# Two-block network with sixteen experts: blocks of 64 in the triangular inverses, part of the convolution and of the masks on GpSimd, output weights loaded into the ring's places

## The chip, the cores and the metric

One core of a Trainium2 chip. The time is device microseconds of one execution, from the median of several. A single profiled execution has its own time; the span is from its first to its last instruction.

## The reference

Two blocks on 256 tokens of width 1024, all in float32. The first (Fourier mixing, neighbourhood attention, an MLP) isn't touched. The second is:

```python
h = rms_norm_2(x, norm_mix_g[l])
p = h @ w_in[l]
q, pc, pr = jnp.split(p, [ATT_WIDTH, ATT_WIDTH + 2 * CONV_WIDTH], axis=-1)
o_att = memory_cross_attention(q, mem_n, w_mk[l], w_mv[l])
o_conv = conformer_conv(pc, conv_w[l], ...)        # gate, 31 taps over 384 channels, layer norm, silu
o_rwkv = rwkv7_bidirectional(pr, shift_mu[l], ...)
x = x + jnp.concatenate([o_att, o_conv, o_rwkv], axis=-1) @ w_out[l]
x = x + expert_choice_ffn(rms_norm_2(x, norm_ffn_g[l]), w_router[l], w_e_gate[l], w_e_up[l], w_e_down[l])
```

The recurrence of `rwkv7_bidirectional`, for six heads of 64, once forward and once backward over the 256 tokens, is

```python
sa = jnp.einsum('bhij,bhj->bhi', state, -kk_t)
state = state * w_t[..., None, :] + sa[..., :, None] * (kk_t * a_t)[..., None, :] + v_t[..., :, None] * k_t[..., None, :]
y_t = jnp.einsum('bhij,bhj->bhi', state, r_t)
```

`expert_choice_ffn` gives each of 16 experts its 32 best tokens; an expert's three matrices are 1024x1024 each.

## The kernel before, in words

The second block runs in `branches`. Its stages overlap, and generators that are advanced in turn (`weave`) write the program in that order; a framework then orders the instructions of each engine.

Projections, attention and convolution (to about 569 us). `w_in` comes in pieces as `raw`, is split into two parts (`split`) by ScalarE and VectorE, and TensorE multiplies (`pw`). Meanwhile the decays, the normalised keys `kkn` and the operands `ex`, `aa` of both directions are made (`decays`, `keys`, `start`). The convolution has 3 x 128 channels in rows and the 256 tokens in columns. Of `cacc[:, 2]` ScalarE makes a product for each tap (`cp`) and TensorE adds them up by a product with the identity (`pconv`, generator `cpe`); `cacc[:, 0]` and `cacc[:, 1]` are 31 taps each on VectorE, a `scalar_tensor_tensor` of 128x256 per tap (`conv`, generator `ct`). GpSimd does little.

The recurrence, in two chunks of 128 tokens, two directions d, and three pairs of heads i, so four 128x128 matrices a pair (2 chunks by 2 heads). `scores(d, i, z)`: products of the operands (`psab`) are masked on VectorE to `LM` (z = 0, kept) or to `LK` (z = 1, one buffer `LM1`, read by `values` for `prh` and `py`). `diagonal` takes the 16x16 blocks of the triangular matrix out (`tm`, then a reduction to `N`), and GpSimd adds the identity. `blocks16` inverts these blocks in 15 steps, one product `prep` and two small VectorE operations each, and spreads the result as a block-diagonal `Gm` of 128 columns. `levels` doubles the blocks twice (16 to 32, 32 to 64): `pp` from the transposed inverse `Tm`, a mask by VectorE to `P`, `pg` to the next `Gm`, and `turn`, four transposes for each of three pairs (`pt`), all as full 128x128 products. A third level joins the two 64 blocks with 64x64 products. `finish(d)` solves (`pu`, `pzz`, `prz`, `py`).

The order: scores of direction 0, then `blocks16(0)` with the scores of direction 1 and convolution, `levels(0)` with `blocks16(1)`, and `levels(1)` with `finish(0)`, the later scores of direction 1 and `bonus`. Then the output weights are read (six loads in `rows0`, `rows1`), and the output products run among the steps of `finish(1)`.

The experts' weights come through a ring of places in SBUF. A place is `wide` (4096 columns) or single (2048). `ring_room` opens places in the space of pools that have closed, `ring_load` issues as many loads on SyncE's queue as there are free places, in the fixed order of the pieces, and `ring_free` gives a place back and loads again. The lists RING, RING0 to RING3 say how many places a point opens and of what size: RING (1, 1, 1, 1) behind the projections, RING0 behind the third level, RING1 behind `finish(1)`, RING2 behind `branches`. A load can't start before the last reader of the space is done.

In the profile's names L277 and L274 are ScalarE copies and activations, L283 VectorE operations of two tensors, L286 those on GpSimd, L290 and L292 operations with scalars, L295 `scalar_tensor_tensor`, L298 products, L302 transposes, L335 weight loads and L1916 the ring's loads.

## Time and profile before

| | us |
|---|---|
| median of 3 runs | 1173.91 (1173.83 to 1174.78) |
| the profiled execution | 1177.93 |
| its span | 1176.2 |
| TensorE busy in the span | 1047.3 (89%) |
| VectorE busy | 509.4 (43%) |
| ScalarE busy | 417.7 (36%) |
| GpSimd busy | 45.7 (4%) |

A share of busy time is a mean over stages with different limits, so the stages are read one by one, by windows. Idle time of an engine counts only where the next engine on the chain waits for it. In the rows, `x` and a number is a count; a matmul in float32 shows as two records per product of full width (a transpose as one).

### The profile page before, as it was taken

The page shows a single profiled execution, that of the slowest core. Times are in us where ns is not written, and L with a number is a line of the kernel's source. Part 1 is how long each engine was busy: PE and PEld are TensorE (multiplying, and loading weights), DVE is VectorE, ACT ScalarE, POOL GpSimd, SP SyncE. Part 2 cuts the span into 40 slices and gives each one's busy share as a digit, 9 for nine tenths or more (in the row PEclk, how much of TensorE's full clock was granted, in tenths as well). Part 3 has the DMA queues.
Part 4 walks back from the last instruction along what each step waited for, and adds up shares of the span by engine and source line. Part 5 has one row for each costly group of instructions (what it writes and reads, how often), then busy time and mean ns, then how long its engine had stood idle before and what let it go on. Part 6 is the DMA issues. An engine that isn't in the chain of part 4 may idle for free.

```text
span 1176.2 us, 19111 instructions
## 1 busy us (share of the span) xinstructions
PE 1047.3 (89%) x8188; PEld 754.7 (64%) x8188; DVE 509.4 (43%) x964; ACT 417.7 (36%) x718; POOL 45.7 (4%) x50
## 2 busy tenths in 40 slices
PE   5999999999999999999989998989877877777776
PEld 4886676899999999898679886434322322222223
DVE  3544356586555555669888555212111111111102
ACT  4542368656444444576324533102000000000003
POOL 0000000021000000101310002000000000000000
PEclk9999999999999999999889998999998798788896
DMA  9874446555555553431300269999999999999995
GB/s 361 359 274 167 179 167 211 176 183 182 205 182 182 192 191 115 158 109 36 143 1 2 109 249 373 425 419 395 429 427 426 426 426 427 427 426 427 427 426 236
DMA packets 34964, 313.86 MB, mean 267 GB/s; under 512 B 4800, under 2 KB 5568, under 8 KB 9152
## 3 DMA queue, kind: packets, MB, share of 16 engines
q1 hardware_dynamic: 34880, 312.65, 66.5%
q8 instruction: 64, 1.05, 0.4%
q14 instruction: 20, 0.16, 0.0%
HBM read 311.59 MB, written 1.05 MB: 266 GB/s over the span
## 4 chain that ended last, share of the span: by engine, by line
PE 69%; DMA 19%; DVE 6%; ACT 4%; issue 1%; POOL 1%; SPq 0%; ACTq 0%; POOLq 0%; DVEq 0%
PE pw L298 22%; DMA ew<-in_w_e_up_dram 12%; PE pd L298 10%; PE acc L298 9%; PE pgu L298 6%; DMA ew<-in_w_e_down_dram 5%; PE pv L298 2%; PE pada L298 2%; PE pg L298 1%; PE pp L298 1%; PE py L298 1%; DVE split L283 1%; PE prep L298 1%; ACT split L277 1%; DMA raw<-in_w_branch_gate_dram 1%; PE pt L302 1%
## 5 line engine op out<-in xcount | busy, mean ns | idle before, releaser
L283 DVE TENSOR_TENSOR split<-raw,split 128x1024 fp32r<-128x1024 f32 (+2 forms) x148 | 177.1, 1203 | 116.2 <-ACT split L277 115.7
L277 ACT ACTIVATE split<-raw 128x1024 fp32r<-128x1024 f32 (+2 forms) x148 | 152.1, 1033 | 133.3 <-PE pw L298 74.4
L298 PE MATMUL pgu<-ew,XE 128*32 128x256 f32 x2048 | 146.5, 430 | 57.4 <-DMA ew<-in_w_e_up_dram 56.6
L298 PE MATMUL pd<-ew,hidT 128*32 128x512 f32 (+2 forms) x560 | 151.5, 594 | 11.2 <-DVE hidT L2140 6.2
L298 PEld LDWEIGHTS pgu<-ew,XE 128*32 128x32 f32 x2048 | 67.7, 120 | 127.8 <-DMA ew<-in_w_e_up_dram 69.5
L298 PEld LDWEIGHTS pd<-ew,hidT 128*32 128x32 f32 x560 | 40.9, 117 | 111.1 <-issue 96.6
L298 PE MATMUL acc<-uh,split 128*128 128x256 f32 x512 | 94.7, 283 | 0.0
L298 PE MATMUL pw<-h2h,split 128*128 128x256 f32 x512 | 92.9, 280 | 0.0
L295 DVE SCALAR_TENSOR_TENSOR hid<-pgu,rs,hid 128x256 f32<-128x256 f32 x16 | 7.7, 484 | 191.2 <-ACT hid L274 191.2
L295 DVE SCALAR_TENSOR_TENSOR ye<-pd,ig,ye 128x512 fp32r<-128x512 f32 (+2 forms) x35 | 24.6, 705 | 144.9 <-ACT ye L274 143.4
L274 ACT ACTIVATE hid<-pgu,rs 128x256 f32<-128x256 f32 x16 | 7.6, 473 | 216.5 <-PE pgu L298 216.5
L274 ACT ACTIVATE ye<-pd,ig 128x512 fp32r<-128x512 f32 (+2 forms) x35 | 22.8, 651 | 166.4 <-PE pd L298 166.3
L298 PEld LDWEIGHTS acc<-uh,split 128*128 128x128 f32 x512 | 80.8, 192 | 0.0
L298 PEld LDWEIGHTS pw<-h2h,split 128*128 128x128 f32 x512 | 79.3, 188 | 0.0
L298 PE MATMUL acc<-ul,split 128*128 128x256 f32 x256 | 72.5, 283 | 0.0
L298 PE MATMUL pw<-h2l,split 128*128 128x256 f32 x256 | 71.4, 279 | 0.0
L298 PE MATMUL pw<-hmh,split 128*128 128x256 f32 x320 | 62.4, 292 | 0.0
L298 PE MATMUL pw<-hxh,split 128*128 128x256 f32 x320 | 61.7, 286 | 0.1
L298 PEld LDWEIGHTS pw<-hxh,split 128*128 128x128 f32 x320 | 50.0, 188 | 9.5 <-issue 8.1
L298 PEld LDWEIGHTS pw<-hmh,split 128*128 128x128 f32 x320 | 51.5, 195 | 1.7 <-DVE u L283 0.5
L298 PEld LDWEIGHTS acc<-ul,split 128*128 128x128 f32 x256 | 49.0, 191 | 0.2 <-DVE ul L283 0.2
L298 PEld LDWEIGHTS pw<-h2l,split 128*128 128x128 f32 x256 | 48.0, 187 | 0.0
(441 smaller groups left out, 1731.3 us busy)
## 6 DMA issues: line engine op xcount, KB each, us to landing
ew<-in_w_e_up_dram SPq DMA_DIRECT2D x28, 2048.0 KB, 18.5
ew<-in_w_e_down_dram SPq DMA_DIRECT2D x28, 2048.0 KB, 19.0
ew<-in_w_e_gate_dram SPq DMA_DIRECT2D x27, 2048.0 KB, 22.0
raw<-in_w_mlp_dram SPq DMA_DIRECT2D x32, 1024.0 KB, 4.8
raw<-in_w_ada_dram SPq DMA_DIRECT2D x24, 1024.0 KB, 5.7
raw<-in_w_in_dram SPq DMA_DIRECT2D x18, 1024.0 KB, 4.9
ew<-in_w_e_gate_dram SPq DMA_DIRECT2D x10, 1024.0 KB, 11.9
raw<-in_w_branch_gate_dram SPq DMA_DIRECT2D x8, 1024.0 KB, 4.8
```

Of the source, the lines that this page charges most:

```text
L274: self.nc.scalar.activation(out, in_, func, **kw)
L277: self.nc.scalar.activation(out, in_, AF.Copy)
L283: self.nc.vector.tensor_tensor(out=out, in0=a, in1=b, op=op)
L295: self.nc.vector.scalar_tensor_tensor(out=out, in0=a, scalar=s, in1=b, op0=op0, op1=op1)
L298: self.nc.tensor.matmul(out, lhsT, rhs, start=start, stop=stop, **kw)
L302: self.nc.tensor.transpose(out, in_, self.ident[0:k, 0:k])
```

## The change

1. `conv_pool` (new): of `cacc[:, 1]` 18 of the 31 taps (from TAPS = 13) are made by ScalarE as products `cq` (two buffers) and added up in `chalf` by GpSimd, during the projections. VectorE's taps of that row begin from `chalf` and stop at 13.
2. `scores` with z = 1: ScalarE copies `psab` and GpSimd multiplies by the mask; `LM1` has two buffers.
3. `diagonal`: only the four 32x32 squares on the diagonal are multiplied, one operation of 32 partitions each, and `N` is one addition of two halves.
4. `Gm`, `Tm` and `P` hold only the 64x64 blocks on the diagonal, stacked (64 columns for a matrix instead of 128). A group of four 128x128 products becomes eight 64x64 products in the two diagonal quadrants. The transposed inverse comes from `P` and the inverse directly (`turned`), beside `pg`, and not by a transpose afterwards; the first is still a product with the identity. In the second doubling the result goes into `whole`, whose off-diagonal quadrant the third level fills.
5. The output weights are loaded packed into the two wide places of RING, now (2, 2), where the scores begin; the expert pieces that were loaded there go out after the pools close (RING_ and RING0). The output products' first steps are advanced in the last eight steps of `levels(1)`.

```diff
-RING, RING0, RING1, RING2, RING3 = (1, 1, 1, 1), (2, 2, 2, 2, 1, 1), (1, 1), (2, 2), (1,)
+TAPS = 13
+
+RING, RING_, RING0, RING1, RING2, RING3 = (2, 2), (1, 1), (2, 2, 2, 2, 1, 1), (1, 1), (2, 2), (1,)
...
+        half = rb.tile([128, 256], F32, name="chalf")
+
+        def conv_pool():
+
+            for t in range(TAPS, 31):
+                x, g = u[:, 1, t:t + 256], cw[:, t, 1:2]
+                if t == TAPS:
+                    self.act(half, x, AF.Identity, scale=g, bias=self.v("conv_b_2", 1))
+                else:
+                    p_ = pj.tile([128, 256], F32, name="cq", tag="cq", bufs=2)
+                    self.act(p_, x, AF.Copy, scale=g)
+                    self.tp(half, half, p_, ALU.add)
+                if t % 2:
+                    yield
...
-        for g in (dec, cd, cd, dec, cd, ma, cd, dec, cd, ma, cd, None, prd, dec, prd, ma, prd, dec, prd, ma,
+        for g in (dec, cd, cd, dec, cd, ma, cd, dec, cd, ma, cd, None, prd, dec, cpool, cpool, prd, ma, cpool, cpool,
+                  prd, dec, cpool, cpool, prd, ma, cpool, cpool, cpool,
...
-        self.ring_load()
+        lent = list(self.free)
+        self.free.clear()
+        rows0, rows1 = {}, {}
+        store = [pool.tile([128, 4096], F32, tag=tag, name="raw", bufs=1) for pool, tag in lent]
+        for n in range(4):
+            rows0[256 * n] = self.wload("w_out_2", 0, 640, 256 * n, 256 * n + 256, raw=store[n // 2][:, n % 2 * 1280:])
+        for n in range(2):
+            rows1[512 * n] = self.wload("w_out_2", 640, 1024, 512 * n, 512 * n + 512, raw=store[n][:, 2560:])
...
-            for i in range(2):
-                self.ts(cacc[:, i], u[:, i, 0:256], cw[:, 0, i:i + 1], ALU.mult, self.v("conv_b_2", i), ALU.add)
-                for t in range(1, 31):
+            for i, n in ((0, 31), (1, TAPS)):
...
+                    self.stt(cacc[:, 1], x, g, half, ALU.mult, ALU.add)
+                for t in range(1, n):
...
-                self.tt(lm.rearrange("p y (j e) t -> p e j y t", e=2)[:, e],
-                        ps[e].rearrange("p (j y t) -> p j y t", j=2, y=2),
-                        mst[d][:, None].to_broadcast([128, 2, 2, 128]), ALU.mult)
+                if z:
+                    self.cpa(o, x)
+                    self.tp(o, o, m, ALU.mult)
+                else:
+                    self.tt(o, x, m, ALU.mult)
...
-            tm = wk2.tile([128, 4, 128], F32, tag="tm", name="tm", bufs=1)
-            self.tt(tm, L, bm[:, None, :].to_broadcast([128, 4, 128]), ALU.mult)
-            nc.vector.tensor_reduce(out=N[d][:, 4 * i:4 * i + 4],
-                                    in_=tm.rearrange("p n (b c) -> p n c b", b=8), op=ALU.add, axis=AX)
+            tm = wk2.tile([128, 4, 32], F32, tag="tm", name="tm", bufs=2)
+            for b in range(4):
+                q = slice(32 * b, 32 * b + 32)
+                self.tt(tm[q], L[q, :, q], bm[q, None, q].to_broadcast([32, 4, 32]), ALU.mult)
+            self.tt(N[d][:, 4 * i:4 * i + 4], tm[:, :, 0:16], tm[:, :, 16:32], ALU.add)
...
-                    for z in range(4):
-                        self.mm(ps[:, z], LM[d, i][:, 0, z], T_[d, i][:, z], True, True)
+                    for z in range(4):
+                        for q in hs:
+                            self.mm(ps[q, z], LM[d, i][q, 0, z, q], T_[d, i][q, z], True, True)
...
-                    for z in range(4):
-                        self.mm(ps[:, z], p1[i][:, z], G[d, i][:, z], True, True)
-                    G[d, i] = next(gms)
-                    self.cpa(G[d, i], ps)
+                    for z in range(4):
+                        for q in hs:
+                            self.mm(ps[q, z], p1[i][q, z], G[d, i][q, z], True, True)
+                    turned(d, i, [p1[i][q] for q in hs], [a] if n else hs)
...
-                turn(d)
-                yield
...
-        self.go(lv)
+        prepare(2)
+        for n, _ in enumerate(lv):
+            if n < 8:
+                next(op)
```

Three places in the order of the two programs show how instructions moved. ScalarE during the projections, around the keys (`cq` are the products for GpSimd, `kkn` the keys, `pr` a projection with its shift), before:

```order
L277 ACTIVATE split_5586<-raw_5526 128x1024
L274 ACTIVATE kkn_5052<-pr_4839,vec_73 128x256
L277 ACTIVATE split_5629<-raw_5627 128x1024
L274 ACTIVATE pr_4839<-pad0_4840,mu01_4820 128x256 x2
L277 ACTIVATE om_4790<-pom_5177 128x256
L274 ACTIVATE kkn_5052<-pr_4839,vec_73 128x256 x2
L274 ACTIVATE LM5_5512<-kkn_5052 128x768
L277 ACTIVATE split_5681<-raw_5627 128x1024
```

The same stretch, with the change:

```order
L280 ACTIVATE kkn_5052<-pr_4839,vec_73 128x256
L280 ACTIVATE cq_5480<-u_4835,vec_73 128x256
L280 ACTIVATE cq_5483<-u_4835,vec_73 128x256
L283 ACTIVATE split_5636<-raw_5576 128x1024
L280 ACTIVATE pr_4839<-pad0_4840,mu01_4820 128x256 x2
L283 ACTIVATE om_4790<-pom_5178 128x256
L280 ACTIVATE cq_5541<-u_4835,vec_73 128x256
L280 ACTIVATE cq_5544<-u_4835,vec_73 128x256
L283 ACTIVATE split_5679<-raw_5677 128x1024
L280 ACTIVATE cq_5547<-u_4835,vec_73 128x256
L280 ACTIVATE cq_5550<-u_4835,vec_73 128x256
L280 ACTIVATE kkn_5052<-pr_4839,vec_73 128x256
```

Pairs of products for GpSimd now stand between the splits and ahead of each `kkn`, and each needs a buffer that a GpSimd addition frees. TensorE in `levels(0)`, from the first turn on (`pt`, `pp`, `pg` as above; `prep` belongs to `blocks16(1)`), before:

```order
L302 MATMUL pt1_6115<-cm_75,Gm0_5810 128x128 x4
L302 MATMUL pt1_6122<-cm_75,Gm1_5811 128x128 x4
L302 MATMUL pt1_6129<-cm_75,Gm2_5812 128x128 x4
L298 MATMUL pp1_6142<-Tm_6120,LM0_5804 128x128 x4
L298 MATMUL pp1_6158<-Tm_6127,LM1_5805 128x128 x4
L298 MATMUL pp1_6172<-Tm_6134,LM2_5806 128x128 x4
L298 MATMUL prep_6151<-N_5799,sel_5786 128x192
L298 MATMUL prep_6165<-N_5799,sel_5786 128x192
L298 MATMUL prep_6179<-N_5799,sel_5786 128x192
L298 MATMUL pg1_6186<-Gm0_5810,P1_6147 128x128 x4
L298 MATMUL prep_6192<-N_5799,sel_5786 128x192
L298 MATMUL pg1_6199<-Gm1_5811,P1_6163 128x128 x4
```

The same place, with the change:

```order
L304 MATMUL pp1_6274<-Tm_6222,LM2_5853 64x64 x8
L304 MATMUL pt1_6301<-P1_6245,Gm0_5863 64x64 x8
L304 MATMUL pt1_6329<-P1_6265,Gm1_5864 64x64 x2
L304 MATMUL prep_6249<-N_5846,sel_5833 128x192
L304 MATMUL prep_6267<-N_5846,sel_5833 128x192
L304 MATMUL prep_6285<-N_5846,sel_5833 128x192
L304 MATMUL pg1_6292<-Gm0_5863,P1_6245 64x64 x8
L304 MATMUL prep_6313<-N_5846,sel_5833 128x192
L304 MATMUL pg1_6320<-Gm1_5864,P1_6265 64x64 x8
L304 MATMUL pt1_6329<-P1_6265,Gm1_5864 64x64 x6
L304 MATMUL prep_6341<-N_5846,sel_5833 128x192
L304 MATMUL pg1_6348<-Gm2_5865,P1_6283 64x64 x8
```

The groups are now of 64x64 products, `pt` stands beside `pg`, and full products (`prep`) alternate with small ones. In the second direction the mask of the first later score was VectorE's, before:

```order
L283 TENSOR_TENSOR P1_6448<-pp1_6443,cr_4817 128x512
L283 TENSOR_TENSOR LM1_6462<-psab_6463,cr_4817 128x2x2x128
L283 TENSOR_TENSOR LM1_6462<-psab_6464,cr_4817 128x2x2x128
L283 TENSOR_TENSOR vv_4838<-vv_4838,pm_6473 128x256
L295 SCALAR_TENSOR_TENSOR bn_6521<-kds_5055,vec_73,pr_4839 128x256
```

ScalarE now has the two copies of that mask, with GpSimd's multiply behind each:

```order
L283 ACTIVATE Tm_6615<-pt1_6606 128x256
L283 ACTIVATE LM1_6647<-psab_6648 128x2x2x128
L283 ACTIVATE kkn_5052<-pu_6639 128x3x128
L280 ACT_TABLE_LOAD
L280 ACTIVATE aa0_5045<-cacc_5056 128x768
L283 ACTIVATE LM1_6647<-psab_6649 128x2x2x128
L280 ACTIVATE gate_5051<-gate_5051,vec_73 128x256
L283 ACTIVATE bt1_5847<-pkt_6690 128x256
```

The second copy stands behind a table load and a sigmoid.

## Rows read from the trace of the kernel before

**Rows 1.** Windows: us, busy us of PE, PEld, DVE, ACT, POOL, then PEclk, DMA share, GB/s.

```profile
549.00:569.00 20.00, 17.06 (x88) 13.57 (x87) 19.17 (x29) 9.19 (x23) 9.73 (x5) 0.91 0.33 128
581.00:617.00 36.00, 32.11 (x184) 26.21 (x185) 29.95 (x78) 9.33 (x21) 4.08 (x3) 0.81 0.01 1
637.00:665.00 28.00, 27.97 (x228) 21.86 (x227) 17.41 (x34) 11.76 (x22) 0.00 (x0) 1.00 0.01 1
665.00:707.00 42.00, 41.78 (x373) 36.82 (x372) 22.20 (x36) 19.53 (x35) 0.00 (x0) 1.00 0.63 251
709.00:1160.00 451.00, 357.65 (x2893) 152.31 (x2895) 66.24 (x160) 45.62 (x81) 7.14 (x7) 0.90 1.00 422
```

**Rows 2.** Timeline of SyncE's issues: start us, us, engine, line, operation, tile, count.

```profile
707.76 1.59 SPq L1916 DMA_DIRECT2D ew<-in_w_e_gate_dram  x2
```

**Rows 3.** Timeline of GpSimd; in square brackets idle time before and its releaser.

```profile
550.72 3.68 POOL L286 TENSOR_TENSOR ex<-pr,ex 128x768 f32<-128x768 f32 x2 [76.03 <-DVE stm L290]
...
572.97 1.27 POOL L1558 TENSOR_TENSOR LM<-LM,cm 128x512 f32<-128x512 f32 x1 [6.06 <-DVE tm L283]
...
710.50 0.73 POOL L286 TENSOR_TENSOR km<-sq 128x256 f32<-128x256 f32 x1 [96.36 <-ACT sq L274]
```

**Rows 4.** Timeline of VectorE, same columns.

```profile
546.58 0.69 DVE L283 TENSOR_TENSOR pad<-pw,rs 128x512 f32<-128x512 f32 x1 [1.36 <-PE pw L298]
...
551.48 3.39 DVE L292 TENSOR_SCALAR LM<-aa,vec,oneka 128x256 f32<-128x256 f32 x3
...
561.93 1.05 DVE L292 TENSOR_SCALAR LM<-aa,vec,oneka 128x256 f32<-128x256 f32 x3
```

**Rows 5.** Chain that ended last, 572 to 617 us: start us, us, what.

```profile
576.72 0.94 DVE N L1556
...
578.64 0.60 DVE tm L283
...
589.76 0.86 PE pconv L298 x4
...
600.08 0.20 DVE g L283
...
600.27 0.39 DVE cacc L295
...
601.50 1.28 DVE LM L283 x2
...
607.79 1.22 DVE Gm L283
...
609.05 2.92 PE pt L302 x12
...
611.97 4.34 PE pp L298 x24
```

**Rows 6.** The same chain, 620 to 633 us.

```profile
620.94 1.31 PE pt L302 x12
...
622.58 0.89 PE pp L298 x8
...
631.20 0.33 PE prep L298 x2
...
632.13 0.52 PE prep L298 x2
```

**Rows 7.** Timeline of TensorE, 64x64 products of the second inverse.

```profile
674.28 1.43 PE L298 MATMUL pp<-Tm,LM 64*64 64x64 f32 x21
...
675.61 0.22 PE L298 MATMUL pg<-Gm,P 64*64 64x64 f32 x1
...
675.61 0.22 PE L298 MATMUL pp<-Tm,LM 64*64 64x64 f32 x1
```

**Rows 8.** Timeline of ScalarE, 656 to 659 us.

```profile
656.38 1.28 ACT L274 ACT_TABLE_LOAD   x1
...
658.82 0.58 ACT L277 ACTIVATE Gm<-pg 128x512 f32<-128x512 f32 x1
```

More of the change, by code (lines that the diff above doesn't have):

```diff
@@ L97, in _const_rwkv, with halves @@
     out = []
+    def halves(m):
+        return np.concatenate([m[0:64, 0:64], m[64:128, 64:128]])
     for d in range(2):
@@ L110, in _const_rwkv @@
             m = (r // (2 * n) == c // (2 * n)) & ((r // n) % 2 == 1) & ((c // n) % 2 == 0)
-            out.append(m | (s == t))
+            out.append(halves(m | (s == t)))
+    out.append(halves(s // 16 == t // 16))
     out.append(s // 16 == t // 16)
@@ L1187, in block2 @@
                     self.logits(x2, 2 * n - 2)
-            self.free.append(self.lent)
+            self.free.extend(self.lent)
             self.ring_load()
@@ L1460, in branches @@
                 next(g, 0)
-        for g in (dec, cd, ma, ky, prd, s0, s1):
+        for g in (dec, cd, ma, ky, prd, s0, s1, cpool):
             assert next(g, 0) == 0
@@ L1528, in branches @@
                [matrices(i) for i in range(3, 6)]]
-        gms = itertools.cycle([(wk if n in (1, 2, 3) else wk0).tile([128, 4, 128], F32, name="Gm%d" % n)
-                               for n in range(7)])
+        whole = [[p.tile([128, 4, 128], F32, name="G%d%d" % (d, n)) for n in range(3)] for d, p in enumerate((wk0, wk))]
+        gms = itertools.cycle([wk0.tile([128, 4, 64], F32, name="Gm%d" % n) for n in range(9)])
         LK = {}
@@ L1615, in blocks16, with turned, levels @@
                 gm = G[d, i] = next(gms)
-                self.tt(gm.rearrange("p n (b c) -> p n b c", b=8),
-                        g[:, 4 * i:4 * i + 4, None, :].to_broadcast([128, 4, 8, 16]),
-                        bm.rearrange("p (b c) -> p b c", b=8)[:, None].to_broadcast([128, 4, 8, 16]), ALU.mult)
+                self.tt(gm.rearrange("p n (b c) -> p n b c", b=4),
+                        g[:, 4 * i:4 * i + 4, None, :].to_broadcast([128, 4, 4, 16]),
+                        bmh.rearrange("p (b c) -> p b c", b=4)[:, None].to_broadcast([128, 4, 4, 16]), ALU.mult)
             yield
-            turn(d)
+            for i in range(3):
+                turned(d, i, [self.ident[q, None, q].to_broadcast([64, 4, 64]) for q in hs])
             yield
+        hs = slice(0, 64), slice(64, 128)
         def v4(ps):
-            return ps.rearrange("p (n t) -> p n t", n=4)
-        def turn(d):
-            for i in range(3):
-                ps = v4(self.pst("pt1", "pw"))
-                for z in range(4):
-                    self.tr(ps[:, z], G[d, i][:, z])
-                T_[d, i] = wk0.tile([128, 4, 128], F32, tag="Tm", name="Tm", bufs=3)
-                self.cpa(T_[d, i], ps)
-        def levels(d):
+            return ps[:, 0:256].rearrange("p (n t) -> p n t", n=4)
+        def turned(d, i, factors, which=hs):
+            ps = v4(self.pst("pt1", "pw"))
+            for z in range(4):
+                for q in which:
+                    self.mm(ps[q, z], G[d, i][q, z], factors[hs.index(q)][:, z], True, True)
+            T_[d, i] = wk0.tile([128, 4, 64], F32, tag="Tm", name="Tm", bufs=3)
+            for q in (which if len(which) == 1 else [slice(0, 128)]):
+                self.cpa(T_[d, i][q], ps[q])
+        def levels(d):
+            a, b = hs if d == 0 else hs[::-1]
+            for i in range(3):
+                nc.gpsimd.memset(whole[d][i][b, :, a], 0.0)
             for n in range(2):
-                ml = lev[d][n][:, None, :].to_broadcast([128, 4, 128])
+                ml = lev[d][n][:, None, :].to_broadcast([128, 4, 64])
                 p1 = []
@@ L1782, in branches @@
         self.free.reverse()
[L1783 to L1790 removed]
         self.ring_load()
[L1792 removed]
+        prepare(1)
         fin = finish(1)
@@ L2027, in experts @@
             self.ring_room(RING3)
-            self.free.extend(self.splits[2:] + [self.orw, self.raws[1], (self.xp, "x")])
+            self.free.extend(self.splits[2:] + [(self.xp, "x")])
             identr = ep.tile([128, 128], F32R, name="identr")
```

65 lines of the change are left out of this document (33 added, 32 removed).

## Prediction

> **What bounds the kernel now.** I read the windows by stage first, then SyncE's timeline, then the chain of waits, then single engines. From 709 us to 1160 the DMA engines are busy for 1.00 of the time at 422 GB/s [rows 1]: the experts' weights stream, and nothing else matters. SyncE's issues wait for places in SBUF, and those that follow the second block stand at 707.76 us [rows 2], behind the block's last reads. Before and after the change the same number of bytes is on the chip by then, because the output weights and the first expert pieces only swap issue slots. So the end is the start of that stream plus bytes over rate: a microsecond taken out of 524 to 707 us is one taken off the kernel, and one added is one added. The question is what bounds that stretch. At 549 to 569 us VectorE is busy for 19.17 of 20 us and TensorE for 17.06; from 581 to 617 TensorE has 32.11 of 36 at a granted clock of 0.81; from 637 to 707 it is busy for 27.97 of 28 and 41.78 of 42 [rows 1]. VectorE, then both in turn, then TensorE alone.
>
> **The change part by part.** Signs are gains (+) and losses (−) in us on that path.
>
> Taps on GpSimd. 18 products go to ScalarE and 17 adds of 128x256 to GpSimd, 16 of them before the attention stage ends. The only row of such an add takes 0.73 [rows 3], so 16 x 0.73 = 11.7 us of GpSimd. VectorE itself makes about as many taps in this stage as before, since those removed come off the end of the list; no VectorE time is saved here. What GpSimd costs VectorE is in two rows: three operations `LM` of 128x256 take 3.39 us at 551.48, beside two GpSimd multiplies that run from 550.72 for 3.68, and 1.05 at 561.93 with GpSimd idle [rows 3, 4]. VectorE had 1.36 us to spare in front of `pad` at 546.58 [rows 4]. Bounds: nothing (each add lies beside work that it does not disturb) and 11.7 − 1.36 = 10.3 (all of it comes back as delay). I take a third, −3.4, nearer the lower end: part of VectorE's work there reads PSUM, and TensorE still has projections to run. Behind the slow operations stand the key and state operands on VectorE, and TensorE's `psab` waits for them; ScalarE's products stand ahead of `kkn` and the splits, on two buffers that GpSimd frees.
>
> The Trainium skill, SBUF — State Buffer, section Who interferes with whom, says that VectorE's second port pair is shared with GpSimd and is an exclusive lock, so that one waits for the whole of the other's instruction. The row of 3.39 against 1.05 agrees. By the rule alone this term would be the −10.3, and the sum 6.9 lower.
>
> Diagonals. A block's diagonal now is `tm` 0.60 and the reduction `N` 0.94 [rows 5]. It becomes four multiplies of 32 partitions and an add. The nearest row is `g` at 0.20 [rows 5], so I estimate 4 x 0.20 + 0.14 = 0.94, a gain of 0.6 each. Three stand on the chain at 572 to 581: +1.8. With them one mask of a later score goes from this chain to GpSimd (half of 1.28, by the pair at 601.50: 0.6), and two taps of 0.39 that filled it [rows 5] are no longer between the links: +3.1 together (bounds 1.8 and 4). Two more diagonals stand in the chain before TensorE's wait for `Gm`, and `Gm` itself, 1.22 at 607.79 [rows 5], has half the columns: 2 x 0.6 + 0.6 = +1.8.
>
> Convolution on TensorE. Three `pconv` products fewer stand behind the transposes: four records, two products, take 0.86 [rows 5], so 3 x 0.43 = +1.3, if TensorE is what is late there (bounds 0 and 1.3).
>
> Inverses by blocks of 64. Per direction before: three turns of 1.31, twelve groups of 0.89 [rows 6], and a third level of 64x64 products; the last stays. 3 x 1.31 + 12 x 0.89 = 14.6. After: 18 groups of eight 64x64 products (16 records), and one turn of half that size. What does such a group take? In one quadrant, 21 records take 1.43 minus the 0.22 in which the last drains, 0.058 each [rows 7]: 16 give 0.93. But at 675.61 a `pg` and a `pp`, which lie in different quadrants, start in the same hundredth [rows 7]; if two run side by side, 16 records give 0.47. I take 0.48: 18 x 0.48 + 1.35 = 10.0, +4.5 per direction, +9.0. The other bound is 18 x 0.93 + 1.35 = 18.1, −3.5 per direction, −7.0.
>
> Against it: each change between a 64x64 product and a full one costs something. `prep` x2 takes 0.33 between full products and 0.52 when 64x64 ones stand on both sides [rows 6]; with the same on the way back I take 0.35 a round trip (0.19 to 0.4). By the order of the two programs there are about 37 more single switches, some 18 round trips: −6.1 (bounds −3.0 and −7.2). Net for the inverses +2.9. The Trainium skill, TensorEngine Tiling (Array Packing), section Key Properties, has both halves: tiles run in parallel, and a change of tiling mode drains the engine. The pair at 675.61 and the 0.52 agree; the page has no price.
>
> Later masks. A `psab` result is now copied by ScalarE (0.58 for that size [rows 8]) and multiplied on GpSimd (1.27 [rows 3]), twice, where VectorE did each half in 0.64 (the pair at 601.50 [rows 5]). In the second direction TensorE is full [rows 1], so `prh`, which reads the mask, becomes a wait. Behind the copies on ScalarE stand `kkn`, the table load of 1.28 [rows 8] and the sigmoid; behind `prh` on TensorE stands all that follows in the levels. Bounds: nothing, as the second buffer lets a mask begin early, and 3 x 2 x 1.27 = 7.6. I take the middle, −3.8. In the first direction the masks lie beside VectorE's chain and are free.
>
> Clock. After the 3.9 us in which TensorE is idle (36 − 32.11 [rows 1]) the twelve transposes at 609.05 take 2.92 where the same at 620.94 take 1.31, and 24 records of `pp` 4.34 instead of 3 x 0.89 [rows 5, 6]: 3.3 us lost at the lower of the two levels, 1.2 GHz. A shorter wait gives back part: +1.5 (bounds 0 and 3.3).
>
> Output weights and products. TensorE has no gap from 665 to 707 us [rows 1], so products moved among the last steps of the second inverse take the place of others: 0. The six loads go out where the scores begin instead of near the end of the second inverse; the expert pieces that had that slot follow at the release, beside a DMA share of 0.63 [rows 1], and land before they are wanted. If they did not, the price is a stall of the stream's head, the last rival below.
>
> Sum: −3.4 + 3.1 + 1.8 + 1.3 + 2.9 − 3.8 + 1.5 = +3.4. The profiled execution took 1177.93 us (span 1176.2 and 1.7 around it), 4.0 above the median 1173.91; it would take 1174.5. On the median: **1170.5 us**.
>
> **Rivals.** *All of it is hidden.* The adds fall beside PSUM reads, masks start early on two buffers, switches cost half and the clock returns: 0 + 3.1 + 1.8 + 1.3 + (9.0 − 3.0) + 0 + 3.3 = 15.5, 1158.4 us. For it: GpSimd was idle for most of the stretch, 9.73 us in 549 to 569 and nothing from 637 [rows 1]. Against: VectorE's idle of 1.36 is a tenth of the adds.
>
> *GpSimd holds VectorE up.* Adds and masks on GpSimd take two SBUF operands each, as those at 550.72 did, and the delay falls on chains that have no slack: −10.3 in the first stage and −7.6 for masks, the rest as above: −10.3 + 10.6 − 7.6 = −7.3, 1181.2 us. It decides once the two together cost more than the 10.6 of the other terms. For it: 3.39 against 1.05. Against: the only masks that TensorE waits for are three.
>
> *The small products do not overlap.* Operand loads or PSUM writes set the pace, 0.93 a group: −7.0 in place of +9.0, sum −12.6, 1186.5 us. For it: one quadrant alone goes at 0.058. Against: the pair at 675.61.
>
> *The block ends earlier and the stream does not.* The pieces whose slot was given up land late, or gains and losses cancel: 1174 us. For it: the loads at the release have more to bring. Against: 0.63 of share until then leaves room.
>
> **How the numbers follow.** Chances: forecast 0.40 (own range 1167.5 to 1173.5), all hidden 0.27, GpSimd in the way 0.15, no overlap 0.06, no shift 0.12. About 0.2%, 2.35 us, is what a measurement of this kernel can tell from no change: below 1171.6 is faster, 1171.6 to 1176.3 the same. Of the forecast's share 0.25 is below, 0.13 within and 0.02 above, by terms that range over more than the margin. Faster 0.25 + 0.27 = 0.52, the same 0.13 + 0.12 = 0.25, slower 0.15 + 0.06 + 0.02 = 0.23. The range, to leave two in ten out, goes from the best case to the GpSimd case: 1158 to 1181.
>
> **What would show it.** In the profile after, SyncE's release that stood at 707.76 stands near 704.3; that one number is the sum. VectorE's operations of 528 to 565 us are longer by about 5 us in all and `psab` starts some 3 us later, or no later at all (adds hidden). A diagonal spans 0.9 us. A group of eight 64x64 products takes 0.5 us and not 0.9. TensorE waits 1 to 1.5 us before each `prh` of the second direction, with GpSimd as the releaser. The transposes after `Gm` start at a higher granted clock. The forecast is wrong if the release moves by more than 6 us either way, or if it moves and the time does not follow.

## The result

The changed kernel takes 1199.78 us (median of 4 runs, 1196.64 to 1202.71) against 1173.87 before: a ratio of 1.0234 with a 95% interval of 1.0214 to 1.0253 (the two medians alone give 1.0221). It is slower by 26 us; the forecast was 3.4 us faster, in a range to 1181. The profiled execution took 1200.81 us, its span 1199.0.

The stretch that the prediction worked on did set the end. The issue that stood at 707.76 us [rows 2] now stands 26.35 us later (SyncE's timeline, start us, us):

```profile
734.11 0.86 SPq L1960 DMA_DIRECT2D ew<-in_w_e_gate_dram  x2
```

The windows of the changed kernel answer to [rows 1] (us, busy us of PE, PEld, DVE, ACT, POOL, then PEclk, DMA share, GB/s). The first four are the same times as before, at which the changed kernel is up to 26 us behind in its work; the last is the stream, moved with its start:

```profile
549.00:569.00 20.00, 17.40 (x80) 13.59 (x80) 15.96 (x35) 13.57 (x31) 6.45 (x2) 0.83 0.00 0
581.00:617.00 36.00, 28.47 (x138) 20.95 (x139) 31.98 (x71) 13.21 (x29) 11.79 (x9) 0.81 0.23 91
637.00:665.00 28.00, 26.66 (x359) 20.71 (x354) 14.06 (x41) 12.09 (x25) 1.27 (x1) 0.94 0.12 40
665.00:707.00 42.00, 40.58 (x486) 33.03 (x484) 15.02 (x32) 18.00 (x44) 7.08 (x5) 0.92 0.39 160
735.00:1185.00 450.00, 357.99 (x2897) 154.60 (x2899) 66.20 (x160) 45.64 (x81) 7.15 (x7) 0.90 1.00 424
```

The stream runs as before, at 1.00 and 424 GB/s. What is lost lies ahead of it. TensorE, busy for 27.97 of 28 us from 637 on before, now has gaps and a lower clock (26.66 of 28, 0.94); GpSimd has 11.79 us in 581 to 617 instead of 4.08.

Stage by stage, by the first start of an operation in the two traces:

| first start of | before | after | later by | added in the stage |
|---|---|---|---|---|
| a masked score (`LM` from `psab`, VectorE) | 569.98 | 583.10 | 13.1 | 13.1 |
| `prep` (TensorE) | 580.82 | 594.81 | 14.0 | 0.9 |
| `pt` of the first turn | 609.05 | 626.54 | 17.5 | 3.5 |
| `pu` of direction 0 | 637.43 | 660.10 | 22.7 | 5.2 |
| `pu` of direction 1 | 678.98 | 704.72 | 25.7 | 3.1 |
| the products with `orw` | 705.73 | 732.20 | 26.5 | 0.7 |

Half of the loss is there before the first score. In the chain that ended last, TensorE's projections led without a break from 520 to 549 us before; in the changed kernel that chain runs through VectorE instead, from its taps to the last split before 549 us.

VectorE in that stage (timeline: start us, us, engine, line, operation, count), before:

```profile
527.98 3.25 DVE L295 SCALAR_TENSOR_TENSOR cacc<-u,vec,cacc 128x256 f32<-128x256 f32 x8
...
539.76 1.67 DVE L295 SCALAR_TENSOR_TENSOR pr<-pad,vec,pr 128x256 f32<-128x256 f32 x4
...
542.74 1.27 DVE L295 SCALAR_TENSOR_TENSOR cacc<-u,vec,cacc 128x256 f32<-128x256 f32 x3
```

With the change:

```profile
527.82 4.73 DVE L301 SCALAR_TENSOR_TENSOR cacc<-u,vec,cacc 128x256 f32<-128x256 f32 x7
...
536.13 2.70 DVE L301 SCALAR_TENSOR_TENSOR cacc<-u,vec,cacc 128x256 f32<-128x256 f32 x3
...
543.42 3.13 DVE L301 SCALAR_TENSOR_TENSOR pr<-pad,vec,pr 128x256 f32<-128x256 f32 x4
```

Seven taps, three taps and four `pr` now take 1.9, 1.4 and 1.5 us longer than as many did before. GpSimd in the same stage, and by the view of one tile the shortest, the mean and the longest of the two `ex` (ns):

```profile
543.73 5.89 POOL L292 TENSOR_TENSOR chalf<-chalf,cq 128x256 f32<-128x256 f32 x6 [2.64 <-ACT cq L280]
...
563.17 9.69 POOL L292 TENSOR_TENSOR ex<-pr,ex 128x768 f32<-128x768 f32 x2 [13.55 <-DVE pr L301]
```

```profile
L292 POOL TENSOR_TENSOR ex<-pr,ex x2: 1800/4863/7926, 563.2 to 571.1; 128x768 f32<-128x768 f32 x2
```

Six adds take 5.89 us, 0.98 each, not the 0.73 of [rows 3]. The two multiplies `ex`, 3.68 in [rows 3], take 9.69, the first of them 7.93: from 563.0 to 569.4 VectorE issues one operation of two SBUF operands behind the other, and the first multiply ends 1.7 us after the last of these. VectorE then waits 4.91 us for GpSimd's next addition and copy, and TensorE 2.6 us for `ex`. TensorE also waits for splits, which it did not before or in e1 below (view of waits: us in total, times, longest):

```profile
PE pw L304 <- DVE split L289: 4.0, 2, 2.5
```

In both places VectorE took its half of the split up 2.4 to 2.5 us after ScalarE's half was done, behind its lengthened taps and `pr`. ScalarE before, at the squares of the keys:

```profile
542.01 0.85 ACT L274 ACTIVATE LM<-kkn 128x768 f32<-128x768 f32 x1
```

With the change:

```profile
547.18 0.51 ACT L280 ACTIVATE cq<-u,vec 128x256 f32<-128x256 f32 x1 [0.36 <-POOL chalf L292]
...
549.74 0.47 ACT L280 ACTIVATE smt<-psm,stm 128x256 f32<-128x256 f32 x1 [1.65 <-DVE stm L296]
...
550.65 0.84 ACT L280 ACTIVATE LM<-kkn 128x768 f32<-128x768 f32 x1
```

A product waits for GpSimd's buffer, the softmax `smt` waits 1.65 us for VectorE, and the squares of the keys (`LM<-kkn`), which start the chain to `psab`, stand behind both, 8.6 us later than before.

The diagonals, on VectorE and on GpSimd:

```profile
585.82 1.47 DVE L289 TENSOR_TENSOR tm<-LM,cr 32x128 f32<-32x128 f32 x5
...
587.22 1.28 DVE L289 TENSOR_TENSOR N<-tm 128x64 f32<-128x64 f32 x1
```

```profile
587.12 1.29 POOL L1598 TENSOR_TENSOR LM<-LM,cm 128x512 f32<-128x512 f32 x1 [6.35 <-DVE tm L289]
```

`N` was to take 0.14 us. It takes 1.28: GpSimd's addition of the identity starts at 587.12, just ahead of it, and both read two SBUF operands. In e10 below, with that addition held back, `N` takes 0.22.

The later masks cost waits, though none of 1 to 1.5 us. From the view of waits from 610 us on:

```profile
PE prh L304 <- POOL LM L292: 2.7, 4, 0.8
```

Two of these four are in the second direction, the other two still in the first. In the second direction the copies of the first mask stand 3.1 us apart on ScalarE (662.71 and 665.78), with the table load and a sigmoid between them. But the masks also cost something in the first direction, where the prediction had them free. GpSimd and VectorE there, with the change:

```profile
604.33 2.67 POOL L292 TENSOR_TENSOR LM<-LM,cr 128x512 f32<-128x512 f32 x2 [8.47 <-ACT LM L283]
```

```profile
604.39 1.48 DVE L301 SCALAR_TENSOR_TENSOR cacc<-u,vec,cacc 128x256 f32<-128x256 f32 x1
...
605.80 1.35 DVE L289 TENSOR_TENSOR Gc<-Gc,g 128x132 f32<-128x132 f32 x1
```

Before, the second of these, a link of VectorE's chain, took 0.29 and such a tap 0.47 to 0.49:

```profile
591.38 0.29 DVE L283 TENSOR_TENSOR Gc<-Gc,g 128x132 f32<-128x132 f32 x1
```

### The profile page after: what moved, and what is told of

Its sections match the earlier page's. It is cut to its first block, busy times and chain, and to the rows that moved or that the text cites. A ratio compares the mean times of both kernels' runs of the same rounds, so it can differ in the third digit from the quotient of the medians.

```text
span 1199.0 us, 19894 instructions
## 1 busy us (share of the span) xinstructions
PE 1055.7 (88%) x8548; PEld 755.5 (63%) x8548; DVE 506.1 (42%) x952; ACT 428.5 (36%) x754; POOL 83.7 (7%) x85
## 3 DMA queue, kind: packets, MB, share of 16 engines
HBM read 311.49 MB, written 1.05 MB: 261 GB/s over the span
## 4 chain that ended last, share of the span: by engine, by line
PE 60%; DMA 23%; DVE 8%; ACT 5%; issue 2%; POOL 2%; SPq 0%; ACTq 0%; POOLq 0%; DVEq 0%
PE pw L304 19%; DMA ew<-in_w_e_up_dram 16%; PE acc L304 9%; PE pgu L304 6%; PE pd L304 6%; DMA ew<-in_w_e_down_dram 3%; DMA ew<-in_w_e_gate_dram 2%; PE pv L304 2%; DVE split L289 2%; PE pada L304 2%; PE py L304 1%; PE prep L304 1%; PE psab L304 1%; PE pg L304 1%; ACT split L283 1%
```

## The experiments

Each kernel was timed against the kernel before on the same chip, and the ratio and its interval are to that kernel. Its median was 1171.76 to 1173.87 on the chips used, so a difference between two experiments from different chips is known to 1 or 2 us only. The label stands ahead of each.

**e1_taps_vec.**

```diff
-            for i, n in ((0, 31), (1, TAPS)):
+            for i, n in ((0, 31), (1, 31)):
...
-                    self.stt(cacc[:, 1], x, g, half, ALU.mult, ALU.add)
```

> The changed kernel with all 31 taps of the second row of the convolution on VectorE again, no products on ScalarE and no adds on GpSimd for it; the rest as changed. In the changed kernel the first masked score starts 13.1 us later than before (583.10 against 569.98 us), and the kernel is 25.9 us longer. Theory T: the taps on GpSimd make these 13 us, so the first mask is back at 570 to 571 us and the time is 1186 to 1188 us. Rival: the 13 us come from the other edits (order of loads, diagonals), and the time stays above 1196 us.

1187.02 us, ratio 1.0127 (1.0105 to 1.015). The first mask starts at 568.83, 14.3 us earlier than in the changed kernel. Theory T holds: the taps cost 12.8 us by the two medians (11.4 with each against the kernel before on its chip), all ahead of the first score.

**e2_short_adds.**

```diff
-                    self.tp(half, half, p_, ALU.add)
+                    self.tp(half[:, 0:1], half[:, 0:1], p_[:, 0:1], ALU.add)
```

> The changed kernel with each of the 17 adds on GpSimd cut to one column of 256 (the convolution's second row is then not computed); ScalarE's 18 products stay. Theory L (the full adds hold VectorE up, and VectorE them): nearly all of the 13 us come back, first mask before 573 us, 1187 to 1190 us. Theory Q (ScalarE's products stand ahead of the splits, keys and softmax): most of the loss stays, first mask at 578 us or later, 1194 to 1200 us.

1195.89 us, ratio 1.0191 (1.0172 to 1.021), first mask at 581.80. That is what theory Q expects, but the framework wrote another order for it: with short adds it put eleven products in a row ahead of the two splits. ScalarE, and TensorE's wait:

```profile
533.90 2.44 ACT L280 ACTIVATE cq<-u,vec 128x256 f32<-128x256 f32 x5
...
536.53 2.88 ACT L280 ACTIVATE cq<-u,vec 128x256 f32<-128x256 f32 x6 [0.19 <-POOL chalf L292]
...
540.78 1.99 ACT L283 ACTIVATE split<-raw 128x1024 fp32r<-128x1024 f32 x2
```

```profile
PE pw L304 <- DVE split L289: 4.5, 1, 4.5
```

So products on ScalarE ahead of a split cost TensorE 4.5 us at one place. In the changed kernel, where they stand in pairs, ScalarE's halves of the splits that TensorE waits for were done in time, as said above; there it was VectorE that came late.

**e3_no_products.**

```diff
-                    p_ = pj.tile([128, 256], F32, name="cq", tag="cq", bufs=2)
-                    self.act(p_, x, AF.Copy, scale=g)
-                    self.tp(half, half, p_, ALU.add)
+                    self.tp(half, half, x, ALU.add)
```

> The changed kernel with the 17 adds on GpSimd reading the convolution's input directly, without ScalarE's 17 products (the second row is then a plain sum). Theory L: the adds still hold VectorE up, 1194 to 1200 us, first mask at 578 us or later. Theory Q: the loss goes with the products, 1186 to 1190 us, first mask before 573 us. A share of each gives a time between.

1197.24 us, ratio 1.0209 (1.0192 to 1.0226), first mask at 577.77. By the time this is theory L; by the trace it is something else. VectorE and GpSimd:

```profile
541.22 0.48 DVE L301 SCALAR_TENSOR_TENSOR cacc<-u,vec,chalf 128x256 f32<-128x256 f32 x1 [5.10 <-POOL chalf L292]
```

```profile
526.64 14.54 POOL L292 TENSOR_TENSOR chalf<-chalf,u 128x256 f32<-128x256 f32 x17 [50.71 <-ACT chalf L280]
```

The framework placed the tap that reads the sum of the adds early in VectorE's order, and VectorE stood 5.10 us until the 17th add was done, with the splits behind it. In the order that the framework wrote for it, either half of the change alone holds the stage up by 8 to 12 us, each by a wait of its own, and the two do not add up.

**e4_masks_vec.**

```diff
-                if z:
-                    self.cpa(o, x)
-                    self.tp(o, o, m, ALU.mult)
-                else:
-                    self.tt(o, x, m, ALU.mult)
+                self.tt(o, x, m, ALU.mult)
```

> The changed kernel with the masks of the later scores on VectorE again (no copies on ScalarE, no multiplies on GpSimd for them), both buffers kept. In the changed kernel TensorE waits for these masks for 3.7 us in all, and VectorE's short operations beside the multiplies take over 1 us longer. Theory M: 4 to 7 us come back, 1193 to 1196 us. Rival: what was late behind the masks is late anyway, within 1.5 us of 1199.8.

1194.24 us, ratio 1.0192 (1.0173 to 1.0211): 5.5 us come back by the two medians (4.2 with each against the kernel before on its chip). The stages from `prep` to `pt` and the two behind it were 3.4, 2.8 and 2.9 us shorter than in the changed kernel. Theory M holds. More than half of this lies ahead of `pu` of direction 0, that is in the first direction's inverse and not at the waits of the second direction.

**e5_taps_masks_vec.** Both edits above together.

> The changed kernel with both the taps and the later masks on VectorE again: what is left of the change are the diagonals, the inverses by blocks of 64, the loads of the output weights and the output products among the last steps. With the taps back the kernel took 1187.0, with the masks back 5.5 us less than the changed one. If the two losses add up, 1180 to 1183 us; if the masks cost more once the taps are gone (the stages behind the first mask were 3.0, 5.6 and 6 us longer than before with the taps back), 1176 to 1180 us. Either way slower than before (1172.6), by the other edits.

1182.14 us, ratio 1.0066 (1.0047 to 1.0084). The losses of taps and masks nearly add up: 17.6 us. Against the trace of e1, the stage from `prep` to `pt` is 27.2 us instead of 33.8 and the next 25.3 instead of 27.2, but the one from there to `pu` of direction 1 is 49.0 instead of 47.5. So here too the masks cost in the first direction.

**e6_no_early_products.** On top of e5:

```diff
-        prepare(2)
-        for n, _ in enumerate(lv):
-            if n < 8:
-                next(op)
+        self.go(lv)
...
-        prepare(1)
+        prepare(3)
```

> As the run with taps and masks on VectorE, and the output products are not advanced among the last eight steps of the second inverse any more, but all from the last solve on, as before. Theory P: from the last solve to the products with the recurrence's output, TensorE is held by the chain of the solve, 27 us with or without those products (26.75 before, 27.5 with the change, where TensorE has 2.5 us of gaps), so products taken out of there lengthen the inverse and shorten nothing; 3.5 to 5 us come back against the run with them. Rival, as predicted: TensorE has no gap in either place, and the time doesn't change (within 1 us).

1178.77 us, ratio 1.0054 (1.0039 to 1.0069): 3.4 us come back by the medians, but 1.7 by the means, and the interval overlaps with that of e5. A loss by the eight products is not clear of noise, and theory P is not shown. In the two traces the stretch from the first mask to the products with `orw` is 140.95 us with them and 141.19 without: the stage from `pu` of direction 0 to `pu` of direction 1 is 4.0 us longer with them, the solve behind it 3.1 us shorter. In the solve of the changed kernel TensorE has 2.5 us of gaps, where it had none before, because the products that used to fill it are used up (window):

```profile
704.72:732.20 27.48, 25.00 (x210) 21.00 (x210) 15.83 (x25) 10.59 (x17) 0.00 (x0) 1.00 0.33 138
```

Without early products, the same stretch is full again, but at a granted clock of 0.89, and 30.19 us long:

```profile
680.05:710.24 30.19, 30.19 (x231) 26.47 (x231) 16.38 (x26) 10.73 (x17) 0.00 (x0) 0.89 0.45 190
```

So with the eight products the solve has gaps and runs at a granted clock of 1.00, and without them it is full and runs at 0.89. The clock is not kept up everywhere with them. In the second inverse of the changed kernel:

```profile
680.00:704.72 24.72, 23.30 (x269) 18.84 (x269) 6.71 (x13) 9.45 (x22) 2.49 (x2) 0.86 0.57 230
```

**e7_old_diagonals.** On top of e6, `diagonal` as before.

> As the run before, and the diagonals are made as before (one masked product of 128x512 and a reduction); left of the change are the inverses by blocks of 64 and the early loads of the output weights. Theory D: the new diagonal takes 4 x 0.29 and an addition of two SBUF operands that stands behind GpSimd's 1.27 us addition, 2.0 to 2.4 us against 1.54, on the chain in five of six; 1.5 to 3 us come back. Rival, as predicted: the old one costs 0.6 each more, 2 to 3 us slower.

1172.46 us, ratio 1.0 (0.9987 to 1.0013): 6.3 us come back, twice what theory D expected. What is left, inverses by 64 and early loads of the output weights, is worth nothing either way. The profiled execution of this kernel took 1180.86 us, far off its median, and is not read here.

**e8_diagonals_alone.** The kernel before with only `diagonal` changed.

> The kernel before with only the diagonals changed (four squares of 32 and one addition). Theory D: 1 to 3 us slower than before, with the additions to N taking 0.8 us or more beside GpSimd's. Rival, as predicted: 2 to 3 us faster.

1178.91 us, ratio 1.0054 (1.004 to 1.0068): 6.1 us slower, the same as in e7. VectorE and GpSimd at the first diagonal:

```profile
570.34 1.16 DVE L283 TENSOR_TENSOR tm<-LM,cr 32x128 f32<-32x128 f32 x4
...
572.15 0.79 DVE L283 TENSOR_TENSOR N<-tm 128x64 f32<-128x64 f32 x1
```

```profile
571.59 1.27 POOL L1559 TENSOR_TENSOR LM<-LM,cm 128x512 f32<-128x512 f32 x1 [6.15 <-DVE tm L283]
```

Four multiplies take 0.29 each, not 0.20, together 1.16 for the 0.60 of before; and `N` ends 0.1 us behind GpSimd's 1.27. A diagonal takes 1.95 us, not the 0.94 forecast, and 1.54 before. Before, the same addition of GpSimd (572.97, 1.27 [rows 3]) lay beside the first of these reductions on VectorE; at the second GpSimd was idle:

```profile
573.50 1.03 DVE L1556 TENSOR_REDUCE N<-tm 128x64 f32<-128x512 f32 x1
...
610.12 1.01 DVE L1556 TENSOR_REDUCE N<-tm 128x64 f32<-128x512 f32 x1
```

The reduction, which reads one SBUF operand, lost nothing beside it.

**e10_add_behind_N.** On top of e8:

```diff
+            s = wk2.tile([128, 1], F32, tag="dg", name="dg", bufs=2)
+            nc.gpsimd.tensor_copy(s, N[d][:, 4 * i, 0:1])
+            with self.in_turn("Pool"):
-            nc.gpsimd.tensor_tensor(out=L, in0=L, in1=self.ident[:, None, :].to_broadcast([128, 4, 128]),
+                nc.gpsimd.tensor_tensor(out=L, in0=L, in1=self.ident[:, None, :].to_broadcast([128, 4, 128]),
```

> The kernel before with the diagonals changed as in the diagonals-alone run (1178.9), and GpSimd's addition of the identity held back until VectorE's addition to N is done (by a copy of one element of N on GpSimd ahead of it). Theory D: N falls from 0.8 us to 0.15 to 0.25; a diagonal is then 1.16 + 0.2 against 1.54 before, and most of the 6 us come back, 1172 to 1175 us. Rival: the loss lies in the four multiplies (1.16 for 0.60) and N's time doesn't matter, 1177 to 1180 us.

1176.15 us, ratio 1.0032 (1.0019 to 1.0044). About 2.8 of 6.1 us come back by the medians (1.7 with each against the kernel before on its chip), between the two expectations. `N` is at 0.22, and the tap behind it pays:

```profile
573.03 0.22 DVE L283 TENSOR_TENSOR N<-tm 128x64 f32<-128x64 f32 x1
...
573.77 1.23 DVE L295 SCALAR_TENSOR_TENSOR cacc<-u,vec,cacc 128x256 f32<-128x256 f32 x1
```

That tap takes 1.23 us where it took 0.48. Held back, GpSimd's addition lies beside the tap instead of beside `N`. Replacing the reduction by an addition took away the cover that it had. What is left of the loss here, 4.4 us, includes the four multiplies, 0.56 us more in each of six diagonals.

**e12_diagonals_look.** The kernel of e8 once more, for a profile.

> The kernel before with only the diagonals changed once more, for a profile: the profiled execution took 1174.8 us where the median was 1178.9 and the slowest 1180.5. If the profile is of a common execution, the 4 us more lie behind the first diagonals, in a stretch in which TensorE runs at the lower clock for longer.

1177.18 us, one execution. First mask to `orw` takes 139.1 us, against 138.4 in the trace of e8 and 135.8 before; the time is spread over the diagonals and the first inverse, and no longer stretch at the lower clock was found. Why the whole is 6 us and the additions on VectorE in six diagonals only some 2.5 stays open.

**e9_inverses_alone.** The kernel before with only the inverses by blocks of 64.

> The kernel before with only the inverses by blocks of 64 (transposed inverse beside pg, gm of 64 columns). In the kernel with old diagonals, taps and masks the first inverse took 24.0 us instead of 28.4, but the stage behind it was 3.6 us longer and TensorE waited there at a lower clock. Theory I: the gain of the first inverse stays and is lost again in the second, where TensorE runs dry behind the small products, so within 2 us of the kernel before (1172.9). Rival, as predicted: 2.9 us faster or more. Rival two: the switches between full and 64x64 products cost more than the products give, 2 to 4 us slower.

1172.84 us, ratio 1.001 (0.9994 to 1.0027): no change. The first inverse takes 24.1 us instead of 28.4, and from `pu` of direction 0 to `orw` there are 72.8 us instead of 68.3. TensorE near the end of the second inverse, and the two windows around it:

```profile
670.19 0.67 PE L303 MATMUL pp<-Tm,LM 64*64 64x64 f32 x8 [0.91 <-ACT Tm L282]
...
671.38 1.61 PE L303 MATMUL pg<-G,P 64*64 64x64 f32 x24 [0.52 <-ACT P L282]
```

```profile
655.00:672.00 17.00, 15.04 (x233) 11.72 (x233) 9.22 (x17) 9.91 (x24) 0.00 (x0) 1.00 0.37 137
672.00:704.05 32.05, 32.05 (x252) 28.05 (x250) 17.89 (x29) 12.48 (x20) 0.00 (x0) 0.89 0.63 256
```

TensorE waits at two places, for the transposed inverse and for `P`, is busy for 15.04 of 17 us, and the granted clock of the next 32 us is 0.89; before, it was busy for 41.78 of 42 us at 1.00 there [rows 1]. What the small products save in one inverse is given back at the other: 2.0 us of waits, and 32 us at 0.89 that would be an estimated 28.5 at 1.00. Theory I holds.

**e11_old_diagonals_look.** The kernel of e7 once more, for a profile.

> The kernel with taps, masks, products and diagonals undone once more, for a profile: the profiled execution took 1180.9 us where the median of twelve was 1172.5. If the profile is of a common execution, the products with the recurrence's output begin at 702 to 704 us (710.6 in that profile), and TensorE doesn't run at the lower clock from 674 to 686 us.

1171.96 us, one execution. The products with `orw` begin at 705.3, and the clock from 672 us on is 0.85: the lower clock is part of a common execution, against what was expected.

**e13_four_products.** On top of e7, four early products where TensorE waits:

```diff
-        self.go(lv)
+        prepare(2)
+        for n, _ in enumerate(lv):
+            if n in (3, 4, 6, 7):
+                next(op)
...
-        prepare(3)
+        prepare(1)
```

> The kernel with taps, masks and diagonals undone (inverses by 64 and early weight loads stay), and four of the output products advanced among the last steps of the second inverse, at the two places where TensorE waits there (1.3 us for the transposed inverse, 0.5 for P), instead of none or eight. Theory W: with none, TensorE waits 1.8 us and then runs at a mean granted clock of 0.85 to 0.9 for 30 us; with eight, the clock stays at 1.00, but the products run out at the end and TensorE has 2.5 us of gaps. With four the clock stays and the end is still filled: 1168 to 1170 us, faster than the kernel before (1171.8 to 1172.9). Rival: the work of TensorE is the same in all three, and the time stays at 1172 to 1173 us.

1166.78 us, ratio 0.9958 (0.994 to 0.9976): faster than both kernels by 0.4%, and by more than expected. TensorE now has products between the small groups, and the same windows as in e9 show it busy and at full clock:

```profile
665.67 0.97 PE L304 MATMUL pw<-om,split 128*128 128x256 f32 x6
...
667.58 0.68 PE L304 MATMUL pp<-Tm,LM 64*64 64x64 f32 x8
```

```profile
655.00:672.00 17.00, 16.46 (x246) 13.71 (x246) 10.97 (x21) 11.19 (x25) 0.00 (x0) 1.00 0.51 182
672.00:704.00 32.00, 31.02 (x256) 26.56 (x256) 19.52 (x30) 11.53 (x18) 0.38 (x1) 1.00 0.56 227
```

From `pu` of direction 1 to `orw` there are 25.8 us, against 30.7 in e11. The four products at the two waits are worth 5.7 us against e7 by the medians, 4.6 with each against the kernel before on its chip. Eight with the old diagonals were not run.

**e14_taps_written_last.** On top of e7, with the taps on ScalarE and GpSimd and their code moved behind both operands (the edit against the changed kernel).

```diff
-        for g in (..., None, prd, dec, cpool, cpool, prd, ma, cpool, cpool, ...
+        for g in (..., None, prd, dec, prd, ma, ..., s1, s1, *[cpool] * 9):
```

> The kernel with masks, products and diagonals undone and the 18 taps on ScalarE and GpSimd, but their code stands behind the keys and both directions' operands, so that they have the least claim. The framework's order still draws most products ahead of the softmax and the last keys, and 13 of 17 adds stand ahead of GpSimd's two multiplies for the operands. Theory L: the adds hold VectorE up wherever they lie in this stage, 6 to 12 us above 1172. Theory Q: with the key products no longer behind ScalarE's, at most 3 us are left, below 1175.5 us.

1179.21 us, ratio 1.0051 (1.0033 to 1.007): 6.8 us above e7 by the medians, 7.8 with each against the kernel before on its chip, in the range of theory L. VectorE and GpSimd at one place (the profiled execution took 1184.46 us, the longest of eight):

```profile
563.38 1.61 DVE L296 TENSOR_SCALAR smt<-smt,stm 128x256 f32<-128x256 f32 x2
```

```profile
563.26 1.58 POOL L292 TENSOR_TENSOR chalf<-chalf,cq 128x256 f32<-128x256 f32 x2
```

Two `smt`, 0.61 together elsewhere, take 1.61 beside GpSimd's adds, so the adds hold VectorE up in this order too. How much of the 6.8 us this is and how much ScalarE's products, which the framework still drew ahead of the softmax and the last keys, this run does not separate; the taps cost 6.0 us more in the order of the changed kernel, by the medians.

## Why the prediction was wrong

| step | forecast, us | measured | by |
|---|---|---|---|
| taps on GpSimd | −3.4 | −11.4 to −12.8 | changed kernel against e1 |
| diagonals alone, five of 0.6 in the +3.1 and +1.8 | +3.0 | −6.3, alone −6.1 | e6 to e7, e8 |
| inverses by 64, with the clock | +2.9 and +1.5 | −1.1 to 0.4 | e9, e7 |
| later masks | −3.8 | −4.2 to −5.5 | e1 to e5, e4 |
| products among the last steps | 0 | −1.7 to −3.4, not clear of noise | e5 to e6 |
| output weights' loads | 0 | 0 | e7, together with the inverses |
| convolution on TensorE | +1.3 | not measured alone | |

**What bounds it.** Right: the issue behind the block moved by 26.35 us and the time by 25.9. The chain inside the block did not stay where it was: up to 549 us it went over from TensorE to VectorE.

**Taps.** This is the step that failed by most: the mechanism was named and its size was not. Taking a third of 10.3 rested on work that reads PSUM; the rows show VectorE's own SBUF operations stretched by 4.8 us at three places alone. The upper bound was too low as well, for two reasons: it counted what GpSimd's adds do to VectorE and not what VectorE does to GpSimd's multiplies (6.0 us at `ex`), and it left the new order of ScalarE at nothing. The Trainium skill, SBUF — State Buffer, section Who interferes with whom, says that the holder of the shared pair blocks the other for a whole instruction; the 7.93 us of the first `ex` agree, in the direction that the prediction did not use, and last over seven of VectorE's operations. By the rule alone the term was the −10.3, which is nearer than the value taken. How the 12.8 us split between the holding up of the two engines by each other and ScalarE's order could not be measured by itself, as the framework wrote another order for each attempt: e14 costs 6.8 us with both in another order, and e2 and e3 lose theirs to waits of their own. The changed kernel's trace says only which engine came late at TensorE's waits: VectorE for the splits (4.0 us), GpSimd for `ex` (2.6), ScalarE for the squares of the keys (1.5). The split of the whole stays open.

**Diagonals.** Wrong in sign. Two sizes failed: a square was priced at 0.20 by the nearest row and takes 0.29, and the addition was priced at 0.14 without asking what runs beside it. GpSimd's addition stood in [rows 3] at 572.97 with VectorE's reduction beside it, and the prediction took the reduction away. Of the 6.1 us, e10 gives 1.7 to 2.8 to `N`'s wait; the operations on VectorE in six diagonals are 2.5 us longer in all, and where the rest comes from stays open.

**Inverses.** The price of a group was about right. From the changed kernel's timeline of TensorE, a group of `pp` and one `prep`:

```profile
639.65 0.68 PE L304 MATMUL pp<-Tm,LM 64*64 64x64 f32 x16
640.26 0.59 PE L304 MATMUL prep<-N,sel 128*128 128x192 f32 x2
640.79 0.68 PE L304 MATMUL pp<-Tm,LM 64*64 64x64 f32 x16
```

From one group to the next it is 1.14 us, against 1.22 in [rows 6] (0.89 + 0.33): 0.61 for the group, 0.53 for `prep`, so the overlap and the price of a switch are both there. The first inverse gains 4.3 us in e9. The clock term was forecast for the wait ahead of the first transposes, and there it came. TensorE from their start, before, behind 4 us in which it was busy for 0.16, and with the change, behind 4.5 us in which it was busy for 2.71:

```profile
609.00:612.00 3.00, 2.95 (x13) 2.51 (x14) 3.00 (x5) 1.19 (x2) 0.00 (x0) 0.50 0.00 0
```

```profile
626.50:629.00 2.50, 2.42 (x68) 2.15 (x70) 2.42 (x6) 1.15 (x3) 1.15 (x1) 1.00 0.03 7
```

The step that failed is the second inverse, whose waits and clock were left at nothing: the shorter groups leave TensorE waiting on the copies between them (0.91 and 0.52 us in e9), and the granted clock behind them is 0.89 for 32 us. In e13, with these waits filled and the clock at 1.00, the blocks of 64 with four early products and the early loads are 5 us faster than the kernel before. Two roundings in the working, 18 x 0.35 = 6.3 and not 6.1, and 14.6 − 10.0 = 4.6 and not 4.5, leave the net of +2.9 as it was.

**Convolution.** Three `pconv` products fewer were to stand behind the transposes. From `prep` to `pt` the traces have 20 records of `pconv` before and 22 with the change, so they are not fewer in that stage, and no run shows the +1.3.

**Masks.** The size was nearly right, 0.4 to 1.7 us short; the place was not. The waits before `prh` of the second direction were to cost all of it, and the first direction was to be free. In e4 and e5 most of what comes back lies in the first direction, where GpSimd's multiplies stretch the small operations of VectorE's chain (1.35 for 0.29) and `prh` waits as well. That the middle of the range came out close is luck.

**Products.** Priced at 0 because TensorE had no gap on either side. No run shows a loss clear of noise, so the 0 may stand. But the two sides are not alike. In the traces the solve takes 26.75 us before, 27.1 to 27.5 with eight products taken out of it, with 2.5 us of gaps, 25.8 with four, and 30.1 to 31.1 with none behind the blocks of 64, where the granted clock is 0.85 to 0.90. What eight take out of it comes back as a gap.

**The rivals.** "GpSimd holds VectorE up" was the right one, priced at 1181 us; with −6.3 for the diagonals in place of the +3.0 that they alone had in it, it would have been 1190.5. `N`'s wait is the same mechanism, the four multiplies are not. The range ended where the delay was counted once, for VectorE by adds and masks.

## What to carry to other kernels

Before moving work to GpSimd, list what VectorE runs at that time and look up in a trace what each operation loses beside GpSimd. Here the reduction lost nothing beside a GpSimd addition (1.03 for 1.01), a tap on two SBUF tensors lost nearly its length (1.23 for 0.48 beside 1.27), and so did `tensor_scalar` on one SBUF tensor (three in 3.39 for 1.05 beside `ex`), so counting operands is not enough. Ask it the other way round too: GpSimd's multiply waited as long as VectorE went on. Before moving filler work into a full stage, ask whether the stage it leaves is bound by a chain; if it is, gaps come in its place. And when an engine's work gets shorter, look for the waits that it uncovers and fill these, no more.

## What was not expected of the hardware

Of two multiplies of 128x768 on GpSimd the first took 7.93 us beside a VectorE that issued operations on two SBUF tensors without a pause, the second 1.80 when VectorE stood still. Before, the two took 3.68 beside three `tensor_scalar`, and there it was VectorE that lost, 3.39 us for 1.05. A `tensor_tensor` of 32 partitions by 128 elements takes 0.29 us on VectorE, so four of them cost twice one of 128 partitions by 512 (0.60). After waits of 0.91 and 0.52 us, among 64x64 products that kept TensorE busy for 15.04 of 17 us, the granted clock was 0.89 over 32 us at full busy share; with four products in these places, and TensorE busy for 16.46 of 17, it stayed at 1.00.
